# The first projection of a two-block layer: w_ada in whole rows, the context normed alone, x loaded last

## The chip, the cores and the metric

The kernel runs on one core of a Trainium2 chip. TensorE (PE, with weight loads PEld), VectorE (DVE), ScalarE (ACT) and GpSimd (POOL) each take their instructions in the order in which they were issued; SyncE (SP) issues most of the DMAs, ACT some. The metric is the device time of one execution in microseconds (us). The kernel before took 3486.61, 3495.49 and 3491.95 us in three runs, median 3491.95 us.

## The reference, cut to what matters

Two transformer blocks run on 512 tokens of width 1024. The first block has a context of 256 tokens beside x, and its norm is modulated by vectors that come from a matrix `w_ada`:

```python
def _modulate(x, g, shift, scale):
    return _rmsnorm(x, g) * (1 + scale) + shift

def _ada(cvec, w_ada, b_ada):                      # w_ada: 1024 x 6144
    mod = jax.nn.silu(cvec) @ w_ada + b_ada
    return jnp.split(mod, N_MOD, axis=-1)
...
    sh1, sc1, ga1, sh2, sc2, ga2 = _ada(c[:, None, :], w_ada, b_ada)
    csh1, csc1, ... = _ada(c_ctx, w_ada, b_ada)
    h, hc = _modulate(x, n, sh1, sc1), _modulate(ctx, n, csh1, csc1)
    ... = _split_in(h @ w_in);  ... = _split_in(hc @ w_in)
    dt_f = softplus(dt_raw[..., :32] + dtb_f)      # the scan's decays come from dt
    a_cs = cumsum(dt * A)                          # within chunks of 128
```

Then come neighbourhood attention, a bidirectional state-space scan (which starts from states of the context), 16 experts, and the second block with three kinds of attention and a gated MLP. All of it is fp32.

## The kernel before, in words

Everything is one program, and each engine's order is the order in which Python issues its instructions. Weights pass through a `Stream`: a raw tile (1 MB of `w_in`, two buffers, tag `raw`) is split into a high part `wh` (ACT, L199) and a low part `wl` (DVE or POOL, L219), in five pairs of buffers. The projection is a row of *steps*. A step is three matmuls (high by high, L330, low activation by high, L331, high by low weight, L332), and `st.fill(c)` issues steps until their costs add up to c: a context step costs 0.33, so `fill(1.0)` issues four and `fill(0.7)` three. `st.defer(n, f)` runs f after n more steps; `st.count` is the number of steps so far.

The stage that the change touches is the first:

- `ada_load` brings the first third of `w_ada` (columns 0 to 2047, 8 MB) as 16 tiles of 512 KB on SP's queue; eight buffers `aw`. The context (2 tiles) and x (4 tiles) come on ACT's queue into `xt`. ACT takes sums of squares (L655), DVE the reciprocal roots (L656, L515 to L520) and the products (L659), PE turns the tiles (L670), ACT and DVE copy them out to `cT` and `xT` (L676, L678).
- PE multiplies silu(c) with `w_ada` (L649). DVE copies the sum to `mod0` (L682), PE turns it (`ptm`, L886), DVE makes the shift and scale `shc`, `gsc` (L892 to L894).
- `modulate(v, ...)` (L683 to L693) makes for each of 8 blocks k: the scaled block (DVE, L686), its high part (ACT, L691: `c_hi`, `h_hi`) and its low part (L692: `c_lo`, `h_lo`). v is 1 for the context and 0 for x.
- Steps, in this order: `ub`, 32 steps of the context (`psc` into `bcT`, with a convolution: ACT L714, 8 DVE instructions L719 per half); `udt`, 8 steps of the context and 8 of x (`psg` into `dtT`); then `xc_unit(0)` to `xc_unit(3)`, 32 context steps each. So x is first needed at step 41.
- The second and last third of `w_ada` come in 16 loads of 1 MB (`ada_load2`, L857, on ACT's queue, three buffers), multiplied by `ada_mm2` (L865) every 10 steps from step 20 on; load i+3 is deferred by 8 steps after product i.
- `dt_ops` turns `dtT` (`dtn`, L759) and makes softplus and `n` = dt A in DVE's small instructions (L760 to L786), one per step; after 16 empty steps PE makes the running sums (`acs`, L766 to L768). For x the chain begins `SX` = 70 steps after `dtT`.

Of the kernel before, what the change touches and what calls it, by code (L numbers as in the profile page):

```python
# [544 lines left out]
ROT = "gsmgsms"  # L545
AQ = 20
AL = 8
SX = 70
VT_ = 't'
VD = 16  # L550
NG = 3
# [16 lines left out]
def first_block(kb, es, after):  # L568
    nc, tc, A = kb.nc, kb.tc, kb.A
    V, S, G, P = nc.vector, nc.scalar, nc.gpsimd, nc.tensor  # L570
# [11 lines left out]
    PS = kb  # L582
# [33 lines left out]
    cT = p0.tile([128, 8, TC], F32, name="cT")  # L616
    raw = ExitStack()
    p00 = raw.enter_context(tc.tile_pool(name="p00", bufs=1, side="right"))
    aw = {}

    def ada_load(kh):
        for j in range(4):
            t = p00.tile([128, 2, 512], F32, tag="aw", bufs=8, name="aw")
            nc.sync.dma_start(t, A["w_ada"][256 * kh:256 * kh + 256, 512 * j:512 * j + 512].rearrange("(k p) f -> p k f", p=128))
            aw[kh, j] = t

    ada_load(0)
    ada_load(1)
    xt = p00.tile([128, 6, D], F32, name="xt")
    for t in (4, 5, 0, 1, 2, 3):  # L630
        src = A["x"][128 * t:128 * t + 128] if t < 4 else A["ctx"][128 * (t - 4):128 * (t - 4) + 128]
        S.dma_start(xt[:, t], src)
    tri = p1.tile([128, 3, 128], F32, name="tri")
    sel = p1.tile([128, 18], F32, name="sel")
    dtv, acs, dte, Eac, cdec = (p1.tile([128, 6, 64], F32, name=n_) for n_ in "dtv acs dte Eac cdec".split())
# [7 lines left out]
    S.activation(sil[:, :, 0:2].rearrange("p k v -> p v k"), cols[:, 112:128].rearrange("p (v k) -> p v k", v=2), AF.Silu)  # L643
    ada_ps = PS.bank([128, 512], F32, "o", "ada")

    def ada_mm(kh):
        for k in range(2):
            for j in range(4):
                P.matmul(ada_ps[32 * j:32 * j + 32], sil[:, 2 * kh + k], aw[kh, j][:, k],  # L649
                         start=kh == 0 and k == 0, stop=kh == 3 and k == 1, skip_group_check=True)  # L650

    ss = p0.tile([128, 6], F32, name="ss")
    junk = xT[:, 0:2].rearrange("p a b -> p (a b)")
    for t in (4, 5, 0, 1, 2, 3):
        S.activation(junk, xt[:, t], AF.Square, accum_out=ss[:, t:t + 1])  # L655
    V.tensor_scalar(ss, ss, 1.0 / D, EPS, op0=ALU.mult, op1=ALU.add)  # L656
    rs = kb.rsqrt(ss, 6, p0)
    for t in (4, 5, 0, 1, 2, 3):
        V.tensor_scalar(xt[:, t], xt[:, t], rs[:, t:t + 1], None, op0=ALU.mult)  # L659
    ada_mm(0)  # L660
    ada_load(2)
    ada_mm(1)
    ada_load(3)
    S.dma_start(tri, A["tri"])
    S.dma_start(sel, A["sel"])
    for n in range(12):
        ps = PS.bank([128, 512], F32, "gsm"[n % 3], "xTp")
        for i in range(4):
            k, t = (2 * n + i // 2, 4 + i % 2) if n < 4 else (n - 4, i)
            P.transpose(ps[:, 128 * i:128 * i + 128], xt[:, t, 128 * k:128 * k + 128], ident)  # L670
        if n < 4:
            o, v = cT[:, 2 * n:2 * n + 2].rearrange("p a b -> p (a b)"), ps
        else:
            o, v = in_time(xT[:, n - 4]), ps.rearrange("p (r g c) -> p r g c", g=8, r=8)
        if n % 2:
            V.tensor_copy(o, v)  # L676
        else:
            S.activation(o, v, AF.Copy)  # L678
    ada_mm(2)
    ada_mm(3)  # L680
    mod0 = p0.tile([128, 512], F32, name="mod0")
    V.tensor_copy(mod0, ada_ps)  # L682
    raw.close()  # L683
    def modulate(v, src, hi, lo, each):
        def scale(k):
            V.tensor_scalar(src[:, k], src[:, k], gsc[:, v, k:k + 1], shc[:, v, k:k + 1], op0=ALU.mult, op1=ALU.add)  # L686
        scale(0)
        for k in range(8):
            if k < 7:
                scale(k + 1)  # L690
            S.activation(hi[:, k], src[:, k], AF.Copy)  # L691
            (G if k % 2 or v else V).tensor_tensor(lo[:, k], src[:, k], hi[:, k].bitcast(F32), op=ALU.subtract)  # L692
            each(k)  # L693


# [25 lines left out]
    def xbc_unit(c0, ch0, out, after):  # L721

        u = Unit([([(0, A["w_in"][512 * i:512 * i + 512, c0:c0 + 512])], 4) for i in range(2)], 512)
        ps = []

        def step(k, j):
            def fn(wh, wl):
                if k == 0 and j % 2 == 0:
                    ps.append(PS.bank([128, 512], F32, "g", "psc"))
                o = ps[-1][:, 256 * (j % 2):256 * (j % 2) + 256]  # L730
                w = slice(128 * j, 128 * j + 128)
                kb.mm3(o, wh[:, w], wl[:, w], *act_c(k), k == 0 and j % 2 == 0, k == 7, skip=True)
# [12 lines left out]
        return st.add(u)

    def dt_ops(t0, nt):

        n = 64 * nt
        tk = slice(t0, t0 + nt)  # L750
        b = {}
        tmp = lambda nm: px.tile([128, 256], F32, tag="dtt", bufs=5, name=nm)[:, :n]
        xr, na, u, d, s = (tmp(n_) for n_ in "x n u d s".split())
        th = lambda v: v.rearrange("p (t h) -> p t h", h=64)

        def turn():
            b["t"] = PS.bank([128, 512], F32, "m", "dtn")[:, :n]
            for t in range(nt):
                P.transpose(b["t"][:, 64 * t:64 * t + 64], dtT[:, 128 * (t0 + t):128 * (t0 + t) + 128], ident[:64, :64])  # L759
            tt(th(xr), th(b["t"]), dtb[:, None, :].to_broadcast([128, nt, 64]), op=ALU.add)  # L760

        def sums():
            ps = PS.bank([128, 512], F32, "m", "acs")
            pv, pt_ = [th(ps[:, 256 * i:256 * i + n]) for i in range(2)]
            a = th(na)
            P.matmul(pv[:, :, :32], tri[:, 0], a[:, :, :32], start=True, stop=True, skip_group_check=True)  # L766
            P.matmul(pv[:, :, 32:], tri[:, 1], a[:, :, 32:], start=True, stop=True, skip_group_check=True)
            P.matmul(pt_, tri[:, 2], a, start=True, stop=True, skip_group_check=True)  # L768
# [14 lines left out]
        ops += [lambda q=q: stt(d, d, 1.0 / q, u, op0=ALU.add, op1=ALU.mult) for q in (13, 11, 9, 7, 5, 3)]
        ops += [lambda: stt(d, d, 1.0, s, op0=ALU.add, op1=ALU.mult),
                lambda: stt(dtv[:, tk].rearrange("p t h -> p (t h)"), d, 2.0, xr, op0=ALU.mult, op1=ALU.add),
                lambda: stt(th(na), dtv[:, tk], -1.0, alog[:, None, :].to_broadcast([128, nt, 64]), op0=ALU.mult, op1=ALU.mult),  # L786
               ] + [None] * 16 + [
                sums, None, None,
                lambda: S.activation(dte[:, tk], dte[:, tk], AF.Exp)]
        return ops  # L790
# [87 lines left out]

    st.stop = True
    ub = xbc_unit(OB, 16, bcT, b_nat)  # L880
    st.add(udt)
    us = [xc_unit(0)]
    st.pump_some(1)
    ptm = PS.bank([128, 512], F32, "t", "ptm")
    for m in range(4):
        P.transpose(ptm[:, 128 * m:128 * m + 128], mod0[:, 128 * m:128 * m + 128], ident)  # L886
    shc = p0.tile([128, 2, 8], F32, name="shc")
    gsc = p0.tile([128, 2, 8], F32, name="gsc")
    for v in (1, 0):
# [2 lines left out]
        V.tensor_tensor(shc[:, v].rearrange("p (j m) -> p j m", m=4), pv[:, 0:2], b4[:, 0], op=ALU.add)  # L892
        V.tensor_tensor(gsc[:, v].rearrange("p (j m) -> p j m", m=4), pv[:, 2:4], b4[:, 1], op=ALU.add)
        V.scalar_tensor_tensor(gsc[:, v], gsc[:, v], 1.0, cols[:, 0:8], op0=ALU.add, op1=ALU.mult)  # L894
    for i in range(3):
        ada_load2(i)
    modulate(1, cT, c_hi, c_lo, lambda k: k in (1, 3, 5) and st.pump_some(1))
    st.stop = False
    st.wait = WAIT
# [2 lines left out]
    kb.rot = ["g", "s"]  # L902
    st.defer(ADA0, lambda: ada_mm2(0))
    S.activation(alog, alog, AF.Exp)
    modulate(0, xT, h_hi, h_lo, lambda k: st.fill(1.0))
    zero.close()
    for g in range(1, 4):
        us.append(xc_unit(g))
# [1718 lines left out]
```

## Time and profile before

| | before |
|---|---|
| median of three runs | 3491.95 us |
| profiled execution, its own time | 3494.57 us |
| its span | 3492.8 us |
| PE busy in the span | 3237.3 us (93%) |
| first 140 us: PE's first projection step | 41.64 us |
| last matmul of the dt unit's x part starts | 72.97 us |
| acs sums of x start | 140.04 us |

Times count from the start of the span. A timeline row has start, duration, engine, line, operation, output<-inputs, the shape and how often (rows that follow each other are merged); what stands in brackets is the idle time before it on that engine and what ended it. A matmul's duration includes its way through the array, so rows overlap: the distance between starts is the pace. In rows of the first `w_ada` product, of the products L865 and of the sums L766 to L768 one matmul of the program is recorded as two. In a row of windows the columns are: window, its length, busy time of PE, PEld, DVE, ACT, POOL (with instructions), TensorE's granted clock as a share of 2.4 GHz, the busy share of the DMA engines and GB/s.

### The profile page before, as it was taken

Reading aid. Unit: us, or ns where it says so; the run is one execution under the profiler, and the core shown is the slowest. Engines: PE = TensorE matmul, PEld = TensorE weight load, DVE = VectorE, ACT = ScalarE, POOL = GpSimd, SP = SyncE. Lnnn points to the kernel's source line nnn. Section 1 sums busy time; section 2 is a strip of 40 time slices with the busy share of each in tenths; the row PEclk is TensorE's granted clock in tenths of the full one; section 3 lists DMA queues with packets and bytes.
Section 4 is the critical chain, followed back from the end, with each engine's and each line's share of the span. In section 5 each row is a group of like instructions: output and inputs, shape, how many; then the busy total and the mean of one; then the engine's idle time right before and its main releaser. Section 6 shows DMA issues by size and latency. Waiting matters only on the chain. (4 is left out here: it accounts for less than half of the span.)

```text
span 3492.8 us, 42198 instructions
## 1 busy us (share of the span) xinstructions
PE 3237.3 (93%) x16445; PEld 2215.0 (63%) x16445; DVE 1631.3 (47%) x3097; ACT 1171.2 (34%) x2066; POOL 568.5 (16%) x380
## 2 busy tenths in 40 slices
PE   7899999999999698988889887999999999999998
PEld 4678876666677443323324223777888877788887
DVE  5745556666554401110111004686544557755444
ACT  4455545454322100000000002554433345543332
POOL 2232213333211100000000002141111103401110
PEclk9999999999999799999999998999999999999999
DMA  8622131222344599999999995211232322123222
GB/s 295 226 64 81 55 97 64 76 79 73 115 163 152 219 403 418 420 421 421 421 421 421 421 421 231 80 46 52 87 95 93 106 72 69 40 67 111 91 87 82
DMA packets 222405, 642.45 MB, mean 184 GB/s; under 512 B 17889, under 2 KB 110169, under 8 KB 170749
## 3 DMA queue, kind: packets, MB, share of 16 engines
q1 hardware_dynamic: 208576, 600.89, 45.2%
q10 hardware_dynamic: 13629, 38.85, 3.1%
q8 instruction: 130, 2.13, 0.2%
q14 instruction: 70, 0.57, 0.1%
HBM read 625.52 MB, written 14.16 MB: 183 GB/s over the span
## 5 line engine op out<-in xcount | busy, mean ns | idle before, releaser
L1911 PE MATMUL hd<-xw,xe 128*64 128x512 f32 x2048 | 464.8, 597 | 63.0 <-DMA xw<-in_w_up_dram 41.7
L219 DVE TENSOR_TENSOR wl<-raw,wh 128x1024 fp32r<-128x1024 f32 (+1 forms) x301 | 372.9, 1253 | 134.3 <-ACT wh L199 129.7
L199 ACT ACTIVATE wh<-raw 128x1024 fp32r<-128x1024 f32 (+1 forms) x349 | 343.2, 1004 | 213.5 <-PE psg L332 131.5
L331 PE MATMUL psg<-HB,wh 128*128 128x512 f32 (+1 forms) x1024 | 388.5, 379 | 8.2 <-DVE HB L429 8.1
L330 PE MATMUL psg<-HA,wh 128*128 128x512 f32 (+1 forms) x1024 | 392.7, 384 | 0.0
L332 PE MATMUL psg<-HA,wl 128*128 128x512 f32 (+1 forms) x1024 | 388.1, 379 | 0.0
L1911 PEld LDWEIGHTS hd<-xw,xe 128*64 128x64 f32 x2048 | 151.1, 137 | 365.8 <-issue 245.2
L1952 PE MATMUL down<-xw,hidT 128*64 128x512 f32 x1024 | 236.5, 596 | 37.8 <-DMA xw<-in_w_down_dram 37.7
L330 PE MATMUL psg<-h_hi,wh 128*128 128x512 f32 x584 | 256.5, 439 | 0.9 <-DVE vsb L1288 0.8
L331 PE MATMUL psg<-h_lo,wh 128*128 128x512 f32 x584 | 237.2, 406 | 1.3 <-POOL h_lo L692 1.3
L332 PE MATMUL psg<-h_hi,wl 128*128 128x512 f32 x584 | 237.3, 406 | 0.0
L331 PEld LDWEIGHTS psg<-HB,wh 128*128 128x128 f32 x1024 | 195.3, 191 | 43.6 <-DVE HB L429 9.8
L332 PEld LDWEIGHTS psg<-HA,wl 128*128 128x128 f32 x1024 | 195.2, 191 | 35.8
L330 PEld LDWEIGHTS psg<-HA,wh 128*128 128x128 f32 x1024 | 195.8, 191 | 33.7
L1952 PEld LDWEIGHTS down<-xw,hidT 128*64 128x64 f32 x1024 | 74.9, 136 | 188.1 <-issue 119.2
L2539 POOL TENSOR_TENSOR va<-va,ga 128x512 f32<-128x512 f32 x44 | 91.2, 2073 | 552.9 <-DVE va L2521 552.6
L1967 ACT ACTIVATE yh<-down,gcol 128x512 fp32r<-128x512 f32 x16 | 11.0, 686 | 489.1 <-PE down L1952 489.1
L219 POOL TENSOR_TENSOR wl<-raw,wh 128x1024 fp32r<-128x1024 f32 (+1 forms) x48 | 113.1, 2360 | 378.7 <-ACT wh L199 378.4
L1923 DVE TENSOR_TENSOR hid<-hid,hd 128x512 f32<-128x512 f32 x32 | 22.0, 688 | 315.6 <-PE hd L1911 315.4
L1985 POOL TENSOR_TENSOR Y<-Y,R 128x512 f32<-128x512 f32 x8 | 9.9, 1273 | 970.8 <-ACT tmp L1984 970.8
L330 PEld LDWEIGHTS psg<-h_hi,wh 128*128 128x128 f32 x584 | 110.9, 190 | 54.0 <-issue 24.2
L332 PE MATMUL psg<-wh,hidl 128*128 128x512 f32 x352 | 139.2, 396 | 0.0
(479 smaller groups left out, 6043.1 us busy)
## 6 DMA issues: line engine op xcount, KB each, us to landing
xw<-in_w_gate_dram SPq DMA_DIRECT2D x128, 1024.0 KB, 19.8
xw<-in_w_up_dram SPq DMA_DIRECT2D x128, 1024.0 KB, 19.8
xw<-in_w_down_dram SPq DMA_DIRECT2D x126, 1024.0 KB, 19.8
raw<-in_w_up_dram SPq DMA_DIRECT2D x176, 256.0 KB, 3.9
raw<-in_w_in_dram SPq DMA_DIRECT2D x34, 1024.0 KB, 5.1
raw<-in_w_in_dram SPq DMA_DIRECT2D x96, 256.0 KB, 3.1
raw<-in_w_down_dram SPq DMA_DIRECT2D x44, 512.0 KB, 3.7
raw<-in_w_in_dram SPq DMA_DIRECT2D x33, 512.0 KB, 5.6
```

Of the source, the lines that this page charges most:

```text
L199: nc.scalar.activation(wh[:, :kn, :nco], src, AF.Copy)
L219: eng.tensor_tensor(wl[:, :kn, :nco], src, wh[:, :kn, :nco].bitcast(F32), op=ALU.subtract)
L330: nc.tensor.matmul(ps, l, r, start=first, stop=False, skip_group_check=skip)
L331: nc.tensor.matmul(ps, l, rh, start=False, stop=False, skip_group_check=skip)
L332: nc.tensor.matmul(ps, lh, r, start=False, stop=last, skip_group_check=skip)
L1911: P.matmul(ps[c][64 * e:64 * e + 64], xe[p // 2][k // 2 % 2][:, 2 * (k // 4) + k % 2, c0:c0 + 64], self.tiles[p, w, k, e][:, 512 * c:512 * ...
L1923: V.tensor_tensor(acts[p, c], acts[p, c], ps[c], op=ALU.mult)
L1952: P.matmul(down[h][64 * e:64 * e + 64], b[:, 64 * e:64 * e + 64], w[:, 1024 * r + 512 * h:1024 * r + 512 * h + 512], start=j == 0 and r == ...
L1967: S.activation(hi, down[h], AF.Copy, scale=gates[p])
L1985: G.tensor_tensor(o, o, R3[:, 512 * h:512 * h + 512], op=ALU.mult)
L2539: G.tensor_tensor(v, v, g[j], op=ALU.mult)
```

## The change

The tiles of `w_ada` become whole rows: eight loads of 1 MB with 8 KB runs, six buffers, all on SP's queue, and their product follows the turning of the context. Only the context is loaded ahead (ACT's queue) and normed alone. x is loaded on SP's queue behind the first two raw tiles of `w_in`, into two of the three buffers of `ada_load2`. Its squares stand on ACT behind the modulation of the context; the norm (`row_norm`), the turning (`x_turn`, one bank of the two with tag `m`) and the copies stand between context steps, and `modulate` of x comes behind all of them. `ada_load2(1)` and `(2)` are issued behind the last `x_turn`. Two groups of 5 and 9 small matmuls (`warm`) stand ahead of the first step. The low part of the context alternates between DVE and POOL. x's dt chain begins 56 steps after `dtT`, and 38 empty steps stand ahead of its sums.

```diff
-SX = 70
+SX = 56
...
-    ada_load(0)
-    ada_load(1)
-    xt = p00.tile([128, 6, D], F32, name="xt")
-    for t in (4, 5, 0, 1, 2, 3):
-        S.dma_start(xt[:, t], src)
+    xt = p00.tile([128, 2, D], F32, name="xt")
+    def ada_load(k):
+        aw.append(p00.tile([128, 4, 512], F32, tag="aw", bufs=6, name="aw"))
+        nc.sync.dma_start(aw[k], A["w_ada"][128 * k:128 * k + 128, :2048].rearrange("p (j f) -> p j f", f=512))
+    for k in range(6):
+        ada_load(k)
+    for t in range(2):
+        S.dma_start(xt[:, t], A["ctx"][128 * t:128 * t + 128])
...
+    row_norm([xt[:, t] for t in range(2)], 4, 2)
...
+    for k in range(8):
+        for j in range(4):
+            P.matmul(ada_ps[32 * j:32 * j + 32], sil[:, k], aw[k][:, j], start=k == 0, stop=k == 7, skip_group_check=True)
+        if k < 2:
+            ada_load(6 + k)
+    kb.warm("m", 5)
+    def x_turn(k):
+        ps = PS.bank([128, 512], F32, "m", "xTp")
+        for t in range(4):
+            P.transpose(ps[:, 128 * t:128 * t + 128], xx[t][:, 128 * k:128 * k + 128], ident)
+        ...  # copied to xT[:, k] by DVE for odd k, by ACT for even k
...
-            (G if k % 2 or v else V).tensor_tensor(lo[:, k], src[:, k], hi[:, k].bitcast(F32), op=ALU.subtract)
+            (G if k % 2 else V).tensor_tensor(lo[:, k], src[:, k], hi[:, k].bitcast(F32), op=ALU.subtract)
...
-               ] + [None] * 16 + [
+               ] + [None] * (16 if t0 else 38) + [
...
     ub = xbc_unit(OB, 16, bcT, b_nat)
+    xx = []
+    for t in range(4):
+        if t % 2 == 0:
+            xa = px.tile([128, 4, 512], F32, tag="aw", bufs=3, name="xa").rearrange("p (t a) c -> p t (a c)", t=2)
+        xx.append(xa[:, t % 2])
+        nc.sync.dma_start(xx[t], A["x"][128 * t:128 * t + 128])
     st.add(udt)
...
+    kb.warm("m", 9)
...
-    for i in range(3):
-        ada_load2(i)
+    ada_load2(0)
     modulate(1, cT, c_hi, c_lo, lambda k: k in (1, 3, 5) and st.pump_some(1))
...
-    modulate(0, xT, h_hi, h_lo, lambda k: st.fill(1.0))
+    for t in range(4):
+        S.activation(junk, xx[t], AF.Square, accum_out=ss[:, t:t + 1])
+        st.fill(0.7)
+    row_norm(xx, 0, 4)
+    for k in range(8):
+        x_turn(k)
+        st.fill(0.6)
+    ada_load2(1)
+    ada_load2(2)
+    modulate(0, xT, h_hi, h_lo, lambda k: st.fill(0.6))
```

The order on ACT in the projection's first part, before, from the last high parts of the context on (`h_hi` is x's high part; `aw` the later thirds of `w_ada`):

```order
L691 ACTIVATE c_hi<-cT 128x256 x2
L904 ACT_TABLE_LOAD
L904 ACTIVATE alog<-alog 128x64
L691 ACTIVATE h_hi<-xT 128x512 x4
L199 ACTIVATE wh<-raw 128x1024
L714 ACTIVATE bcT<-psc,cols,cw 128x256 x2
```

The same place now, to x's first high parts (`xa` is x, `xTp` its turned blocks):

```order
L694 ACTIVATE c_hi<-cT 128x256 x2
L913 ACT_TABLE_LOAD
L913 ACTIVATE alog<-alog 128x64
L915 ACTIVATE xT,ss<-xa 128x1024 x4
L683 ACTIVATE xT<-xTp 128x8x8x8
L199 ACTIVATE wh<-raw 128x1024
L717 ACTIVATE bcT<-psc,cols,cw 128x256 x2
L683 ACTIVATE xT<-xTp 128x8x8x8
L199 ACTIVATE wh<-raw 128x1024
L683 ACTIVATE xT<-xTp 128x8x8x8
L199 ACTIVATE wh<-raw 128x1024
L683 ACTIVATE xT<-xTp 128x8x8x8
```

The four squares of x and the four copies now stand between the context's high parts and x's. ACT's next rows now (`aw` are loads of the later thirds, `bcT` the output of `ub`):

```order
L199 ACTIVATE wh<-raw 128x1024
L860 DMA aw_507<-in_w_ada_dram 128x2048
L860 DMA aw_509<-in_w_ada_dram 128x2048
L860 DMA aw_511<-in_w_ada_dram 128x2048
L694 ACTIVATE h_hi<-xT 128x512 x2
L717 ACTIVATE bcT<-psc,cols,cw 128x256 x2
L741 ACT_TABLE_LOAD
L741 ACTIVATE bcT<-bcT 128x1024
L199 ACTIVATE wh<-raw 128x1024
L694 ACTIVATE h_hi<-xT 128x512 x3
```

Three loads of `w_ada` stand behind the last copy and one more split of a raw tile; between x's second and third high part stand the convolution of `ub`'s second half, a table load, a silu and a split.

On PE the eight turnings of x stand between the steps of `ub`. The first comes behind 12 steps, and the last is followed by four steps and the product that reads `aw_509` (the second of the three loads above):

```order
L678 MATMUL xTp<-ident,xa 128x128 x4
L330 MATMUL psc<-c_hi,wh 128x256
L331 MATMUL psc<-c_lo,wh 128x256
L332 MATMUL psc<-c_hi,wl 128x256
L330 MATMUL psc<-c_hi,wh 128x256
L331 MATMUL psc<-c_lo,wh 128x256
L332 MATMUL psc<-c_hi,wl 128x256
L678 MATMUL xTp<-ident,xa 128x128 x4
```

Two steps stand between each two turnings. Before, PE's program began thus (`pt` are small vectors), and all 48 transposes of context and x came in one piece ahead of the second half of the product:

```order
L637 MATMUL pt<-ident,va 128x128
L638 MATMUL pt<-ident,vb 128x120
L649 MATMUL ada<-aw,sil 32x512 x16
L670 MATMUL xTp<-ident,xt 128x128 x48
L649 MATMUL ada<-aw,sil 32x512 x16
L886 MATMUL ptm<-ident,mod_290 128x128 x4
```

What moved is x's 32 transposes, from ahead of the product's second half into the steps. In DVE's order x's dt chain, before, is spread over a convolution, products for the context's states and a split:

```order
L783 SCALAR_TENSOR_TENSOR d_624<-d_624,u_623 128x256 x4
L839 TENSOR_TENSOR xd_1131<-xn_1126,ddc_297 128x512
L839 TENSOR_TENSOR xd_1133<-xn_1126,ddc_297 128x512
L784 SCALAR_TENSOR_TENSOR d_624<-d_624,s_625 128x256
L785 SCALAR_TENSOR_TENSOR dtv_127<-d_624,x_621 128x256
L839 TENSOR_TENSOR xd_1158<-xn_1153,ddc_297 128x512
L839 TENSOR_TENSOR xd_1160<-xn_1153,ddc_297 128x512
L786 SCALAR_TENSOR_TENSOR n_622<-dtv_127,alog_303 128x256
```

Now it ends ahead of them:

```order
L786 SCALAR_TENSOR_TENSOR d_640<-d_640,u_639 128x256 x6
L787 SCALAR_TENSOR_TENSOR d_640<-d_640,s_641 128x256
L788 SCALAR_TENSOR_TENSOR dtv_119<-d_640,x_637 128x256
L789 SCALAR_TENSOR_TENSOR n_638<-dtv_119,alog_233 128x256
L219 TENSOR_TENSOR wl_1104<-raw_1042,wh_1103 128x1024
```

From the turning of x's dt to the first `acs` matmul PE's order has 113 rows before and 180 now (some 22 steps more).

## Rows read from the trace of the kernel before

**Rows 1.** Waits of PE from 0 to 140 us: total, times, longest.
```profile
PE psc L331 <- POOL c_lo L692: 2.7, 5, 1.0
PE acs L766 <- DVE n L786: 7.0, 1, 7.0
```

**Rows 2.** Timeline of PE: the end of the first product, the first step.
```profile
35.11 1.90 PE L649 MATMUL ada<-aw,sil 128*32 128x512 f32 x10 [1.49 <-DMA aw<-in_w_ada_dram]
41.64 0.58 PE L330 MATMUL psc<-c_hi,wh 128*128 128x256 f32 x1 [3.19 <-ACT c_hi L691]
```

**Rows 3.** Windows of the first 35 us.
```profile
0.00:5.00 5.00, 0.00 (x0) 0.00 (x0) 0.00 (x0) 0.00 (x0) 0.19 (x4) 1.00 0.60 184
5.00:10.00 5.00, 0.91 (x2) 0.36 (x2) 0.75 (x3) 0.00 (x0) 0.00 (x0) 1.00 1.04 397
30.00:35.00 5.00, 3.62 (x28) 1.20 (x26) 1.20 (x2) 0.60 (x1) 0.00 (x0) 1.00 1.06 388
```

**Rows 4.** Timeline of ACT: squares, last context part, table load, alog.
```profile
11.84 1.28 ACT L643 ACT_TABLE_LOAD   x1 [11.84 <-DMA xt<-in_ctx_dram]
14.42 1.06 ACT L655 ACTIVATE xT<-xt 128x1024 f32<-128x1024 f32 x1
15.60 1.06 ACT L655 ACTIVATE xT<-xt 128x1024 f32<-128x1024 f32 x1
51.72 0.42 ACT L691 ACTIVATE c_hi<-cT 128x256 fp32r<-128x256 f32 x1 [1.72 <-DVE cT L686]
53.46 0.26 ACT L904 ACTIVATE alog<-alog 128x64 f32<-128x64 f32 x1
```

**Rows 5.** Timeline of DVE: the norm, mod0, one convolution.
```profile
20.72 0.17 DVE L656 TENSOR_SCALAR ss<-ss 128x6 f32<-128x6 f32 x1 [12.42 <-ACT xT L655]
23.14 4.07 DVE L659 TENSOR_SCALAR xt<-xt,rs_y 128x1024 f32<-128x1024 f32 x6
37.05 0.69 DVE L682 COPY mod<-ada 128x512 f32<-128x512 f32 x1 [5.67 <-PE ada L649]
59.55 3.98 DVE L719 SCALAR_TENSOR_TENSOR bcT<-psc,cw,bcT 128x255 f32<-128x255 f32 x8 [0.23 <-ACT bcT L714]
```

**Rows 6.** Timeline of POOL and PE: block 5's low part, a product, two matmuls.
```profile
48.83 0.73 POOL L692 TENSOR_TENSOR c_lo<-cT,c_hi 128x256 fp32r<-128x256 f32 x1 [0.68 <-ACT c_hi L691]
55.44 1.06 PE L865 MATMUL ada<-aw,sil 128*32 128x512 f32 x8
54.05 0.28 PE L331 MATMUL psc<-c_lo,wh 128*128 128x256 f32 x1
54.17 0.28 PE L332 MATMUL psc<-c_hi,wl 128*128 128x256 f32 x1
```

**Rows 7.** One line's DMAs (L857, 30 to 110 us).
```profile
DMA to landing us min/median/max: 6.1/6.8/9.1
```

**Rows 8.** Timeline of ACT, DVE, POOL, PE: silu, x's blocks, turnings, dt's end.
```profile
75.38 1.28 ACT L738 ACT_TABLE_LOAD   x1 [4.13 <-DVE bcT L719]
76.68 1.06 ACT L738 ACTIVATE bcT<-bcT 128x1024 f32<-128x1024 f32 x1
64.02 0.64 ACT L691 ACTIVATE h_hi<-xT 128x512 fp32r<-128x512 f32 x1 [3.03 <-DVE xT L686]
63.45 0.54 DVE L686 TENSOR_SCALAR xT<-xT,gsc,shc 128x512 f32<-128x512 f32 x1
54.84 1.28 POOL L692 TENSOR_TENSOR h_lo<-xT,h_hi 128x512 fp32r<-128x512 f32 x1 [1.66 <-ACT h_hi L691]
78.76 0.60 PE L817 MATMUL bct<-ident,bcT 128*128 128x128 f32 x4
72.97 0.41 PE L332 MATMUL psg<-h_hi,wl 128*128 128x512 f32 x1
```

**Rows 9.** Windows: steps from 75.6 us on, then the sums of x.
```profile
75.60:94.00 18.40, 17.70 (x143) 14.30 (x141) 14.15 (x28) 11.71 (x15) 7.15 (x3) 1.00 0.94 340
140.04:143.00 2.96, 2.96 (x12) 2.78 (x13) 2.85 (x6) 0.00 (x0) 0.00 (x0) 0.50 0.23 44
```

More of the change, by code (lines that the diff above doesn't have):

```diff
@@ L618, in first_block @@
     p00 = raw.enter_context(tc.tile_pool(name="p00", bufs=1, side="right"))
[L619 to L625, printed above, removed]
-    ada_load(0)
-    ada_load(1)
-    xt = p00.tile([128, 6, D], F32, name="xt")
-    for t in (4, 5, 0, 1, 2, 3):
-        src = A["x"][128 * t:128 * t + 128] if t < 4 else A["ctx"][128 * (t - 4):128 * (t - 4) + 128]
-        S.dma_start(xt[:, t], src)
+    xt = p00.tile([128, 2, D], F32, name="xt")
+    aw = []
+    def ada_load(k):
[5 more added lines that the diff above has]
+        S.dma_start(xt[:, t], A["ctx"][128 * t:128 * t + 128])
     tri = p1.tile([128, 3, 128], F32, name="tri")
@@ L644, in first_block @@
     ada_ps = PS.bank([128, 512], F32, "o", "ada")
[L646 to L650, printed above, removed]
     ss = p0.tile([128, 6], F32, name="ss")
     junk = xT[:, 0:2].rearrange("p a b -> p (a b)")
-    for t in (4, 5, 0, 1, 2, 3):
-        S.activation(junk, xt[:, t], AF.Square, accum_out=ss[:, t:t + 1])
@@ L656, in first_block, with row_norm @@
[L656 to L663, printed above, removed]
+    for t in range(2):
+        S.activation(junk, xt[:, t], AF.Square, accum_out=ss[:, 4 + t:5 + t])
     S.dma_start(tri, A["tri"])
     S.dma_start(sel, A["sel"])
-    for n in range(12):
+    def row_norm(x, t0, n):
+        v = ss[:, t0:t0 + n]
+        V.tensor_scalar(v, v, 1.0 / D, EPS, op0=ALU.mult, op1=ALU.add)
+        rs = kb.rsqrt(v, n, p0)
+        for t in range(n):
+            V.tensor_scalar(x[t], x[t], rs[:, t:t + 1], None, op0=ALU.mult)
@@ L667, in first_block @@
+    row_norm([xt[:, t] for t in range(2)], 4, 2)
+    for n in range(4):
         ps = PS.bank([128, 512], F32, "gsm"[n % 3], "xTp")
         for i in range(4):
[L669 to L672, printed above, removed]
-        else:
-            o, v = in_time(xT[:, n - 4]), ps.rearrange("p (r g c) -> p r g c", g=8, r=8)
@@ L675, in first_block @@
-        if n % 2:
+            P.transpose(ps[:, 128 * i:128 * i + 128], xt[:, i % 2, 256 * n + 128 * (i // 2):256 * n + 128 * (i // 2) + 128], ident)
+        o = cT[:, 2 * n:2 * n + 2].rearrange("p a b -> p (a b)")
+        if n % 2:
+            V.tensor_copy(o, ps)
+        else:
+            S.activation(o, ps, AF.Copy)
+    for k in range(8):
[3 more added lines that the diff above has]
+            ada_load(6 + k)
@@ L676, in first_block @@
+    kb.warm("m", 5)
[3 more added lines that the diff above has]
+            P.transpose(ps[:, 128 * t:128 * t + 128], xx[t][:, 128 * k:128 * k + 128], ident)
+        o, v = in_time(xT[:, k]), ps.rearrange("p (r g c) -> p r g c", g=8, r=8)
+        if k % 2:
             V.tensor_copy(o, v)
@@ L678, in first_block @@
             S.activation(o, v, AF.Copy)
-    ada_mm(2)
-    ada_mm(3)
     mod0 = p0.tile([128, 512], F32, name="mod0")
```

## The prediction

> **What bounds the kernel now.** The page's engine shares give PE 93% of the span, so I read first where PE waits. The waits of PE up to 140 us say that it waited 7.0 us in one place, for DVE's last instruction of x's dt chain, and 2.7 us in five places for the context's low parts [rows 1]. The timeline of PE shows the start: the first product of `w_ada` still waits for a DMA at 35.11, and the first projection step starts at 41.64, behind ACT's first high part [rows 2]. The windows show why: from 5 us on the DMAs move 388 to 397 GB/s [rows 3], so until 35 us the queues are the limit, and x's 2.1 MB are among their bytes. The reader should see that x's squares and turnings cost nothing there, because PE waits for `w_ada` anyway. From 75.6 us on PE is busy 17.7 of 18.4 us [rows 9], and its list of waits has little else until the 7 us. What matters is thus how much earlier the steps start, whether x is ready when its steps come, and whether the wait at 133 us goes.
>
> I count the chain from M, the start of DVE's copy `mod0`: 37.05 us [rows 5]. From there the order up to the context's last high part is nearly the same in both kernels.
>
> **Part 1: the start.** x's four tiles (2.1 MB) no longer go ahead of `w_ada`; at 388 GB/s [rows 3] that is 5.4 us. Against it stands a new wait: loads 7 and 8 need the buffers of the first two products, and these come behind the context's norm and its 16 transposes. The context has landed by 11.84 at the latest (ACT's table load was let go then) [rows 4]; two squares at 1.18 us (the distance of two of them) [rows 4] take 2.4, DVE's twelve small instructions 2.4 and two products at 0.68 (4.07 over 6) 1.4 [rows 5], four groups of transposes 2.4 (0.60 each [rows 8]) and the first product 1.1 [rows 6]: load 7 is issued at 21.5. Six tiles, the context and the small loads are 7.75 MB; 0.92 MB are through at 5 us and 397 GB/s from then on [rows 3], so the queue runs empty at 22.2. A load that takes 6.1 us at best [rows 7], 2.7 of it for its megabyte, leaves it empty for up to 2.7 us, or not at all. I take half of that: M comes 4.0 us earlier (2.7 to 5.4), at 33.0.
>
> The rate in rows 3 was reached with 512 KB issues, eight in flight. The Trainium skill (DMA: Bandwidth & Descriptors, Bandwidth) counsels batches of 1 MiB and more and gives 425 GB/s for one long transfer. By that rate the 9.8 MB would be there about 2 us earlier, and the sum below would be 2 us less; the trace has shown no such rate in this stretch, and I keep its own.
>
> **Part 2: x's path.** ACT's order decides it. The context's last high part ends at 52.14, which is M+15.1, and `alog` at M+16.7 [rows 4]; both rest on the same alternation of splits, scalings and high parts as now, and giving DVE every second low part leaves that alternation as it is. Behind `alog` stand x's four squares, 4.7 us: M+21.4. DVE then needs 2.4 us for the small instructions and 4 x 0.68 = 2.7 for the products: M+26.5. PE, meanwhile, has 12 steps. They need the low parts of blocks 0 to 5; block 5's was ready at 49.56 [rows 6], M+12.5, so PE is done at about M+13 and waits some 13 us in front of the first turning, a wait that wasn't there. (x itself lands in time: two raw tiles, x and one load of `aw` are 5.2 MB, at 388 GB/s 13.5 us from about M on, and the squares can't start before M+16.7. The tile of the dt unit, now queued on SP behind x, is used on ACT only behind x's first copy.) The small matmuls ahead of the first step only fill time in which PE waits.
>
> The loop has 8 turnings at 0.60 [rows 8], 16 steps at 0.35 (three matmuls 0.117 apart) and one product of 1.06 [rows 6], 11.5 us. After the wait of 7 us the granted clock stood at 0.50 for 3 us [rows 9], which cost half of them; after 13 us I put 1.5 us down for it, and 0.5 for the turning that finds its bank not yet emptied, since DVE's convolution of 3.98 us [rows 5] stands between two copies. The loop ends at M+40.
>
> Then comes a second new wait. The loads of `aw` for the second and third product are issued on ACT behind a split that waits for the loop's last step (1.04 more) and behind a load for the fourth product: the one that PE needs next goes out at M+41.5, and PE stands in front of its product at M+40.7. A load takes 6.1 to 9.1 us, median 6.8 [rows 7]; with one megabyte ahead of it I take 8.0 (6.1 to 11.8, which is 9.1 and the 2.7 of the other). PE goes on at M+49.5. Product and two steps, at half clock, are 2 us: M+51.5. ACT's half of the convolution takes 0.5, DVE's 3.98 [rows 5]: M+56. On ACT table load, silu and split come first, 1.28 + 1.06 + 1.04 = 3.4 [rows 8, 2 to 4], then x's third high part, 0.64 [rows 8]: M+60. For the remaining blocks DVE has per pair two scalings of 0.54 [rows 8] and a low part, taken as 0.69 from the copy of the same shape [rows 5]: 1.8; three pairs 5.4, and POOL ends with a low part of 1.28 [rows 8]. The last matmul of the dt unit starts at about M+67.
>
> Before, it started at 72.97, M+35.9 [rows 8]. So x's path costs 31.3 us, of which the earlier M takes off 4.0: **+27.3**. PE can't cover this: only 40 steps, 14 us, don't need x, and all else stands behind in PE's order.
>
> **Part 3: the decays.** x's chain starts 14 steps earlier and the sums stand 22 steps later behind its start, at 0.35 about 8 us more room than before, when DVE was 7.0 late [rows 1]. That wait goes; with it the 3.0 us at half clock behind it, 1.5 us [rows 9]. DVE's work stays the same and is now ahead of the convolution. **-8.5**, bounded by 0 (DVE as late as before, since it too was held up) and -8.5.
>
> **Part 4: what is caught up.** Behind the dt unit PE had 0.7 us idle in 18.4 [rows 9]; little can be made good there. I take **-1.5** (0 to -3). Behind 140 us nothing changes but the time at which it starts.
>
> **Sum.** 27.3 - 8.5 - 1.5 = +17.3 on the profiled execution's own 3494.57 us: 3511.9. That execution stood 2.6 us above the median of the runs, 3491.95; against the median the time is **3509 us**. The bounds: M from 2.7 to 7.4 us earlier (the last by the faster queue), the load from 6.1 to 11.8, the clock's 3 us or none, the rest as above: +9 to +25, 3501 to 3517.
>
> **Rivals.**
> A. x is in time, and the change is faster. If neither new wait shows, the start brings 4.0, the decays 8.5 and the five waits for low parts 2.7 [rows 1], and the 32 transposes add 4.8 to PE: -10.4, 3482 us. For it speaks that x lands early and that DVE and ACT have idle time in the stretch; against it ACT's order, in which the squares can't start before M+16.7. It decides from the point at which the two waits together stay under some 10 us; I count 13 and 9, and x's late high parts on top.
> B. The second wait is short: if the load lands in 6.1 us and the two scalings and POOL's parts run beside the silu, x is ready about 10 us sooner: +7, 3499 us. For it: the first load in its queue is the fourth product's, and it may have landed by then. Against: the convolution, the table load and the silu stay in front.
> C. The decays bring nothing: DVE, held up by the convolutions behind the dt unit, is late for the sums as before. +26, 3518 us. For it speaks DVE's 14.2 busy of 18.4 us in the stretch [rows 9]; against it that its chain now stands ahead of that work.
>
> **How the numbers follow.** Forecast 0.62, A 0.12, B 0.16, C 0.10. 0.3% (10.5 us) is what a measurement of this kernel can tell from no change. The forecast lies above +10.5 for 0.55 of its 0.62; B for 0.05; C wholly: slower 0.70. No change: 0.07 of the forecast, 0.11 of B, 0.04 of A, 0.22. Faster: the rest of A, 0.08. The range from 3490 to 3519 holds the forecast, B and half of C; the forecast's own is 3501 to 3517.
>
> **What would show it.** In the profile after: first step at about 37.6 (M+4.6); PE idle some 13 us in front of the first `xTp`, put down to DVE's product of x; a wait of some 9 us for `aw` in front of the second product L868; the last matmul of the dt unit at about 100 us; no wait of 7 us in front of `acs`, and the sums of x at about 162 us. I am wrong if ACT's squares run earlier than the context's last high part, if the product doesn't wait for its load, or if the wait for `acs` is still there.

## The result and the profile after

The changed kernel took 3514.46 us (median of four runs, 3512.76 to 3518.72) against 3491.15 us for the kernel before (3486.61 to 3495.49): 0.69% slower, ratio 1.0069, 95% interval 1.0056 to 1.0082. The forecast of 3509 us was 5.5 us too low. The profiled execution took 3518.72 us (span 3516.8), 24.15 us more than that of before.

The waits of PE from 0 to 180 us (total, times, longest) answer to [rows 1]:

```profile
PE xTp L678 <- DVE xa L656: 11.1, 3, 10.7
PE ada L868 <- DMA aw<-in_w_ada_dram: 7.8, 1, 7.8
PE psg L330 <- ACT h_hi L694: 3.6, 1, 3.6
PE psg L331 <- DVE h_lo L695: 1.9, 1, 1.9
PE xn L838 <- ACT xc L741: 2.4, 2, 2.0
PE psc L332 <- POOL wl L219: 1.8, 1, 1.8
PE psc L331 <- DVE c_lo L695: 1.1, 1, 1.1
```

The wait of 7.0 us for `acs` is gone, and no row is left for it. In its place stand the two forecast waits, 10.7 us in front of x's first turning and 7.8 us in front of the second product of `aw`, and behind them two that the forecast had not priced apart: 3.6 us for x's third high part and 1.9 us for its low part.

The windows of the start (columns as in [rows 3]), and one further on:

```profile
0.00:5.00 5.00, 0.00 (x0) 0.00 (x0) 0.00 (x0) 1.28 (x1) 0.19 (x4) 1.00 0.62 216
5.00:10.00 5.00, 0.45 (x1) 0.18 (x1) 0.00 (x0) 0.00 (x0) 0.00 (x0) 1.00 1.02 414
10.00:15.00 5.00, 0.46 (x1) 0.18 (x1) 0.75 (x3) 1.26 (x3) 0.00 (x0) 1.00 1.02 410
15.00:20.00 5.00, 0.00 (x0) 0.00 (x0) 2.22 (x13) 1.15 (x2) 0.00 (x0) 1.00 1.02 422
20.00:25.00 5.00, 4.26 (x24) 3.41 (x28) 2.42 (x4) 1.20 (x2) 0.00 (x0) 1.00 0.24 87
97.00:102.00 5.00, 4.78 (x11) 3.19 (x11) 4.76 (x7) 1.71 (x3) 2.58 (x2) 0.50 0.86 297
```

From 5 to 20 us the queues run faster than in [rows 3], at 410 to 422 GB/s for 397, and then they have next to nothing to move from 20 to 25 us (87 GB/s). ACT's and DVE's timelines show why, and where M (the copy `mod0`) now stands:

```profile
13.02 1.04 ACT L646 ACTIVATE xT<-xt 128x1024 f32<-128x1024 f32 x1
16.19 1.06 ACT L646 ACTIVATE xT<-xt 128x1024 f32<-128x1024 f32 x1 [2.03 <-DMA xt<-in_ctx_dram]
36.81 1.06 ACT L199 ACTIVATE wh<-raw 128x1024 fp32r<-128x1024 f32 x1 [12.35 <-DMA raw<-in_w_in_dram]
94.11 1.14 ACT L694 ACTIVATE h_hi<-xT 128x512 fp32r<-128x512 f32 x2
33.94 0.69 DVE L685 COPY mod<-ada 128x512 f32<-128x512 f32 x1 [8.82 <-PE ada L670]
37.90 1.23 DVE L219 TENSOR_TENSOR wl<-raw,wh 128x1024 fp32r<-128x1024 f32 x1 [3.27 <-ACT wh L199]
```

The context's second tile lands near 16 us; in before both had landed by 11.84 [rows 4]. The norm, the turnings and the first two products, which free the buffers for the last two loads, come later by that. SP's own waits say the same:

```profile
SPq L624 <- PE ada L670: 9.7, 2, 9.3
```

PE's timeline reads as follows; the first row answers to [rows 2], and the others follow x's path to its end.

```profile
40.71 0.38 PE L330 MATMUL psc<-c_hi,wh 128*128 128x256 f32 x1 [3.08 <-ACT c_hi L694]
59.37 1.05 PE L678 MATMUL xTp<-ident,xa 128*128 128x128 f32 x2 [10.72 <-DVE xa L656]
82.42 1.08 PE L868 MATMUL ada<-aw,sil 128*32 128x512 f32 x4 [7.81 <-DMA aw<-in_w_ada_dram]
94.77 0.51 PE L330 MATMUL psg<-h_hi,wh 128*128 128x512 f32 x1 [3.58 <-ACT h_hi L694]
97.22 0.80 PE L331 MATMUL psg<-h_lo,wh 128*128 128x512 f32 x1 [1.94 <-DVE h_lo L695]
104.62 0.42 PE L332 MATMUL psg<-h_hi,wl 128*128 128x512 f32 x1
```

The last row is the end of the dt unit: 31.65 us later than in before [rows 8]. The whole is 24.15 us longer, so 7.5 us come back behind it; they come back within this stage, since its last PE work (the last `stc` of the table below) is 23.7 us later.

### The profile page after: what moved, and what is told of

Its sections match the earlier page's. It is cut to its first block, busy times and chain, and to the rows that moved or that the text cites. A ratio compares the mean times of both kernels' runs of the same rounds, so it can differ in the third digit from the quotient of the medians.

```text
span 3516.8 us, 42242 instructions
## 1 busy us (share of the span) xinstructions
PE 3240.3 (92%) x16473; PEld 2220.3 (63%) x16473; DVE 1626.6 (46%) x3113; ACT 1169.9 (33%) x2064; POOL 561.3 (16%) x376
## 5 line engine op out<-in xcount | busy, mean ns | idle before, releaser
L332 PEld LDWEIGHTS psg<-HA,wl 128*128 128x128 f32 x1024 | 195.0, 190 | 35.9
```

The costliest lines, as they stand in the source:

```text
L332: nc.tensor.matmul(ps, lh, r, start=False, stop=last, skip_group_check=skip)
```

## The experiments

Twelve kernels ran, each at least five times. The ratio is to the kernel before, run on the same chip in the same series. The last column is the start of the last product of the context's states (`stc`, the last PE work of this stage) in the profiled execution, of which there is one for each kernel. Behind it all kernels run the same program, for 3293 to 3301 us, while whole runs of one kernel differ by up to 14 us. How much the last two columns scatter was not measured apart, but after, e2, e3, e4, e6, e10 and e12 have the same program up to `mod0`, and it starts between 33.9 and 35.5 us in them: differences of 1 to 2 us there say little. Differences to after are given between medians of different series; by the ratios they are up to 3.5 us larger or smaller.

| kernel | median, us | ratio to before (95%) | mod0 at | last stc at |
|---|---|---|---|---|
| before | 3488.73 to 3491.70 (four series) | 1 | 37.1 | 192.7 |
| after | 3514.46 | 1.0069 (1.0056 to 1.0082) | 33.9 | 216.4 |
| e1 decays alone | 3486.18 | 0.9989 (0.9981 to 0.9998) | 37.4 | 187.0 |
| e2 decays undone | 3519.73 | 1.0094 (1.0081 to 1.0106) | 35.5 | 224.0 |
| e3 products late | 3510.23 | 1.0058 (1.0045 to 1.0071) | 34.6 | 211.7 |
| e4 x's dt behind ctx | 3516.15 | 1.0074 (1.0062 to 1.0086) | 34.5 | 216.5 |
| e5 context first | 3510.01 | 1.0052 (1.0040 to 1.0064) | 29.3 | 210.6 |
| e6 turnings late | 3515.00 | 1.0068 (1.0056 to 1.0080) | 34.1 | 212.7 |
| e7 decays, low parts | 3483.77 | 0.9980 (0.9971 to 0.9990) | 37.2 | 185.5 |
| e8 rows alone | 3499.82 | 1.0022 (1.0014 to 1.0031) | 44.4 | 198.3 |
| e9 = e3 and e5 | 3503.64 | 1.0040 (1.0027 to 1.0053) | 29.6 | 207.2 |
| e10 x not normed | 3504.88 | 1.0049 (1.0035 to 1.0062) | 34.9 | 205.1 |
| e11 short runs | 3516.57 | 1.0073 (1.0060 to 1.0086) | 32.8 | 214.3 |
| e12 as e4, sums kept | 3515.45 | 1.0072 (1.0059 to 1.0084) | 35.0 | 215.8 |

### The decays: e1 and e2

e1, on the kernel before:

```diff
-SX = 70
+SX = 56
...
-               ] + [None] * 16 + [
+               ] + [None] * (16 if t0 else 38) + [
```

> The kernel before with only the move of x's decays (SX 56, 38 empty steps ahead of x's sums). Theory: PE's wait of 7.0 us in front of the sums goes, with the 3 us at half clock behind it: 6 to 8.5 us less than before, 3483 to 3485 us, and no wait above 1 us in front of acs. Rival: DVE is held up by its convolutions and is as late as before, or the wait comes back elsewhere: 3490 to 3493 us.

e2, on the kernel after: the same two lines back.

> The kernel after with x's decays put back (SX 70, 16 empty steps). Theory: the wait in front of x's sums is there again, 5 to 7 us with half clock behind it: after plus 5 to 8.5 us, 3519.5 to 3523 us. Rival: PE's waits ahead of the dt unit have given DVE the time it lacked, so the sums come in time anyway: 3513 to 3516 us.

e1 is 0.11% faster (ratio 0.9989; 3486.18 for 3490.31 us), its last `stc` 5.7 us earlier. e2 is 5.3 us above after, its last `stc` 7.6 us later, of which 1.6 are there at `mod0` already. In e2 the wait stands in front of the sums as before, and as long:

```profile
PE acs L769 <- DVE n L789: 7.0, 1, 7.0
```

So the theory's mechanism holds in both kernels and e2's rival falls: PE's waits ahead of the dt unit give DVE no time, since its chain begins behind them. The size is 4 to 6 us (4.1 and 5.3 by the medians, 5.7 and 6.0 at the last `stc`) and not 8.5, though e2's ratio taken alone would give 8.7. The waits of e1 behind 76 us show what takes a part back:

```profile
PE xn L835 <- ACT xc L738: 3.1, 2, 2.0
PE psc L332 <- POOL wl L219: 1.8, 1, 1.8
PE psg L331 <- DVE wl L219: 1.4, 1, 1.4
```

In before PE waited 1.1 us for `xc` and not at all for POOL's `wl` there. With PE no longer held up 7 us, these two come late by 2.0 and 1.8 us more. DVE's `wl` costs less than before; its 1.4 us in e1 lie behind the last `stc`.

### The start: e5, e11, e8

e5, on after: `va`, `vb` and the context go to SP's queue, ahead of `w_ada`.

```diff
-    S.dma_start(va, A["vec_a"])
-    S.dma_start(vb, A["vec_b"])
+    nc.sync.dma_start(va, A["vec_a"])
+    nc.sync.dma_start(vb, A["vec_b"])
...
+    for t in range(2):
+        nc.sync.dma_start(xt[:, t], A["ctx"][128 * t:128 * t + 128])
     for k in range(6):
         ada_load(k)
-    for t in range(2):
-        S.dma_start(xt[:, t], A["ctx"][128 * t:128 * t + 128])
```

> The kernel after with the two small loads va and vb and the context moved from ACT's queue to SP's, ahead of w_ada. Theory: the context landed late (second tile near 16 us) because the 8 KB rows of w_ada on the other queue took the rate; with it first in the same queue it is there by 8 us, the first two products free their buffers before the queue runs dry, and the stretch at 87 GB/s (20 to 25 us) goes: mod0 starts 3 to 5 us earlier than 33.9, and the whole is 2.5 to 5 us shorter than after, 3509.5 to 3512 us. Rival: the megabyte ahead of w_ada costs as much as the dry stretch, or mod0 comes earlier and x, behind ACT's and DVE's work, does not: 3513.5 to 3516 us.

The theory held: the context's first square starts at 5.86 us and its second at 7.21, the dry stretch is gone, `mod0` comes 4.6 us earlier and the time is 4.5 us below after. What `va` and `vb` have in it, which moved with the context and stand ahead of its squares, was not taken apart. ACT's timeline and the window that was dry:

```profile
7.21 1.06 ACT L646 ACTIVATE xT<-xt 128x1024 f32<-128x1024 f32 x1 [0.19 <-DMA xt<-in_ctx_dram]
```

```profile
20.00:25.00 5.00, 3.00 (x16) 0.36 (x16) 0.00 (x0) 0.00 (x0) 0.00 (x0) 0.70 1.01 421
```

The waits of 10.7, 7.5 and 3.6 us behind it are those of after: the chain from M on moves as a whole.

e11, on after: shorter runs in four times as many loads, all else the same.

```diff
-        nc.sync.dma_start(aw[k], A["w_ada"][128 * k:128 * k + 128, :2048].rearrange("p (j f) -> p j f", f=512))
+        for j in range(4):
+            nc.sync.dma_start(aw[k][:, j], A["w_ada"][128 * k:128 * k + 128, 512 * j:512 * j + 512])
```

> The kernel after with each of the eight w_ada loads cut into four of 256 KB (runs of 2 KB instead of 8 KB), same tiles, same queue, same order. Theory: the long runs on SP's queue took the rate from ACT's; with short ones va lands by 6 us instead of 8.9, the context by 12 to 14 instead of 16, the loads 7 and 8 are issued earlier and the stretch at 87 GB/s shrinks: mod0 1.5 to 3 us earlier and the whole 1 to 3 us below after, 3511.5 to 3513.5 us. Rival: the six megabytes queued ahead matter and not the run length: va at 8.9 us and mod0 at 34 as in after, 3514 to 3517 us.

Half right. PE gets `va` at 5.24 us, and the context's second square starts at 11.88 instead of 16.19, so the way SP's loads are cut decides who is served; the packets in the last section speak for the length of the runs and not the number of loads. But the total rate falls, and takes most of it back:

```profile
5.00:10.00 5.00, 0.91 (x2) 0.36 (x2) 0.75 (x3) 1.86 (x3) 0.00 (x0) 1.00 0.94 329
15.00:20.00 5.00, 3.56 (x16) 3.24 (x16) 2.45 (x6) 1.04 (x2) 0.00 (x0) 1.00 1.05 375
20.00:25.00 5.00, 5.00 (x42) 1.27 (x43) 0.69 (x1) 0.16 (x1) 0.00 (x0) 1.00 0.99 353
```

`mod0` is 1.1 us earlier and the last `stc` 2.1, hardly more than the scatter, and the whole time, 3516.57 us, can't be told from after.

e8, on before: only `w_ada` in whole rows, four buffers of 1 MB for eight of 512 KB.

```diff
+        aw.append(p00.tile([128, 4, 512], F32, tag="aw", bufs=4, name="aw"))
+        nc.sync.dma_start(aw[k], A["w_ada"][128 * k:128 * k + 128, :2048].rearrange("p (j f) -> p j f", f=512))
...
+    for k in range(4):
+        ada_load(k)
...
+            if k < 4:
+                ada_load(4 + k)
```

> The kernel before with only the loads of w_ada changed: eight of 1 MB in whole rows (8 KB runs), four buffers, SP's queue; x and the context on ACT's queue and normed together, as before. Theory: w_ada's rows take the rate from ACT's queue, the context and x land later than before (x's last tile by 4 us or more) and the norm, the turnings and with them the loads 5 to 8 come later: mod0 at 38 to 42 instead of 37.1, the whole 1 to 4 us above before, 3491.5 to 3494.5 us. Rival: the total rate is what counts, and it is higher (410 to 420 GB/s for 397): mod0 1 us earlier, 3489 to 3490 us.

The mechanism was right and its size too small: 0.22% slower, 8 us. ACT's row of the square of x's last tile shows it; in before it started at 19.54 us.

```profile
27.51 1.06 ACT L654 ACTIVATE xT<-xt 128x1024 f32<-128x1024 f32 x1 [2.62 <-DMA xt<-in_x_dram]
```

The norm waits for all six tiles, the products for the norm and the loads 5 to 8 for the products: `mod0` is 7.3 us later. Whole rows alone are thus a loss in this order of work, though the rate from 5 to 30 us is 410 to 423 GB/s.

### x's path: e10, e3, e9, e6, e4, e12

e10, on after:

```diff
     for t in range(4):
-        S.activation(junk, xx[t], AF.Square, accum_out=ss[:, t:t + 1])
         st.fill(0.7)
-    row_norm(xx, 0, 4)
```

> The kernel after without x's four squares, reciprocal roots and products: x goes into its turnings as it is loaded (that part of the computation is left out). Theory: the wait of 10.7 us in front of the first turning is these 9.8 us on ACT and DVE, and all of x's path behind it moves up as a whole: after minus 8 to 11 us, 3503.5 to 3506.5 us, with the first xTp at 49 to 51 us and the waits for the load and for h_hi as in after. Rival: the convolution, the load or the splits hold x's path anyway, and the waits behind grow by what is saved: 3511 to 3515 us.

The first turning starts at 49.5 us instead of 59.4, the last `stc` is 11.3 us earlier and the time 9.6 us below after. The waits behind stay:

```profile
PE ada L868 <- DMA aw<-in_w_ada_dram: 7.8, 1, 7.8
PE psg L330 <- ACT h_hi L694: 2.4, 1, 2.4
PE psg L331 <- DVE h_lo L695: 2.1, 2, 1.9
```

So the norm of x on ACT and DVE, behind the context's high parts, costs its full length (10 us), and nothing on the way makes it good. This shows the forecast's first wait directly, and that it is on the path.

e3, on after:

```diff
-ADA = 10
-ADA0 = 20
+ADA = 9
+ADA0 = 36
...
-AL = 8
+AL = 7
```

> The kernel after with the first product of the second third of w_ada at step 36 instead of 20 and the next ones every 9 steps instead of 10 (loads 7 steps behind a product instead of 8). Theory: PE no longer stands 7.8 us in front of a load; the convolution, the silu and x's third high part come as much earlier: after minus 6 to 9 us, 3505.5 to 3508.5 us. Rival: x's high and low parts are late by ACT's and DVE's own work, and the waits of 3.6 and 1.9 us for h_hi and h_lo grow by what the load gave: 3512 to 3515 us.

Between the two: 4.2 us below after, the last `stc` 4.7 us earlier. The wait for the load is gone, but two others grew:

```profile
PE psg L330 <- ACT h_hi L694: 6.5, 1, 6.5
PE ada L868 <- DVE modx L871: 3.8, 1, 3.8
PE psg L331 <- DVE h_lo L695: 1.7, 1, 1.7
```

```profile
86.99 1.14 ACT L694 ACTIVATE h_hi<-xT 128x512 fp32r<-128x512 f32 x2
```

The convolution and x's third high part came 7 us earlier (86.99 for 94.11), and the dt unit ended at 97.52 instead of 104.62: 7.1 us, as the theory said for x's path. PE reached its place 10 us earlier, x's part was ready 7 us earlier, so the wait for `h_hi` grew by 3. The later place of the products then cost 3.8 us in front of the last third's first product, whose bank DVE copies out late (`modx`).

e9 is e3 and e5 in one kernel.

> e5_ctx_first and e3_products_late together. Theory: the late context (4.5 us) and the wait for the load in x's loop (4.2 us) are separate, and their gains add: 3505 to 3507 us, still some 22 us above e7, which is what is left of x's late path. Rival: the second only moved because x was late by the first, and together they bring little more than one: 3509 to 3511 us.

3503.64 us, 10.8 below after, last `stc` 9.2 us earlier where the sum of the two is 10.5: they nearly add. 20 us are left over e7; x's norm, which e10 takes out, is half of that, and what the rest is was not taken apart.

e6, on e3:

```diff
-        st.fill(0.7)
+        st.fill(2.0)
...
         x_turn(k)
-        st.fill(0.6)
+        st.fill(0.3)
```

> The kernel of e3_products_late with 28 steps instead of 12 ahead of the first turning of x, and one step instead of two behind each turning. Theory: the 10.7 us in front of the first turning are ACT's and DVE's (the squares behind the context's high parts, the norm, the products); PE can fill 5.6 us of them with steps, and x's path behind them is 5 to 6 us shorter: 5 to 8 us less than e3, 3502 to 3505.5 us; the wait in front of the first xTp falls from 10.7 to about 5 us. Rival: the turnings were paced by DVE's and ACT's copies and not by the steps between them, and the wait for h_hi (6.5 us in e3) grows by what PE saves: 3508 to 3511.5 us.

My theory fell. The first turning comes at 68.2 us, 8.8 later than in after, behind a wait of 12.2 us. ACT's and DVE's rows show what the steps brought with them:

```profile
62.68 1.06 ACT L199 ACTIVATE wh<-raw 128x1024 fp32r<-128x1024 f32 x1 [2.94 <-DMA raw<-in_w_in_dram]
```

```profile
56.84 3.98 DVE L722 SCALAR_TENSOR_TENSOR bcT<-psc,cw,bcT 128x255 f32<-128x255 f32 x8 [6.85 <-ACT bcT L717]
60.73 2.51 DVE L219 TENSOR_TENSOR wl<-raw,wh 128x1024 fp32r<-128x1024 f32 x1
63.78 1.23 DVE L219 TENSOR_TENSOR wl<-raw,wh 128x1024 fp32r<-128x1024 f32 x1 [0.53 <-ACT wh L199]
64.92 0.16 DVE L653 TENSOR_SCALAR ss<-ss 128x4 f32<-128x4 f32 x1
```

A step isn't PE's alone: issued between the squares, 28 of them put a convolution and the splits of the next weights on ACT and DVE ahead of the norm, and one split waits 2.9 us for its raw tile. The rival had a part in it too: with one step between two turnings, PE waited 4.1 and 2.4 us for DVE's and ACT's copies. The last `stc` is 1.0 us behind e3's, the median 4.8, so there is no gain by either, and how much is lost stays open. PE's idle time couldn't be filled by steps that use the engines for which it waited.

e4, on after: x's eight steps in a unit of their own behind `xc_unit(0)`; e12 is e4 with `SX = 24`.

```diff
+    udx = Unit([([(0, A["w_in"][:, ODT:ODT + 128])], 8)], 128)
...
-    kb.group_b(udt, 0, act_t, T, ev_dtx)
+    kb.group_b(udx, 0, act_t, T, ev_dtx)
...
     us = [xc_unit(0)]
+    st.add(udx)
```

> The kernel after with x's 8 steps of the dt unit put behind the context steps of xc_unit(0) (with a load of their weights of their own), so that x is first needed at step 73 instead of 41. Theory: the waits for h_hi (3.6 us) and h_lo (1.9 and 0.4 us) and the half clock there go: after minus 6 to 9 us, 3505.5 to 3508.5 us; the waits of 10.7 and 7.8 us stay. Rival: the waits only move, to the sums of x or to the convolutions of xc_unit(0) that x's low parts now meet on DVE: 3512 to 3517 us.

> As e4_x_dt_behind_ctx, but x's chain begins 24 steps behind dtT instead of 56, so that x's sums stand at the same step as in after (in e4 they came 32 steps later). Theory: with x first needed at step 73 the waits for h_hi and h_lo go and nothing takes their place: 3506 to 3509 us. Rival, which e4 spoke for: x's scalings and low parts meet the context's dt chain on DVE, PE waits some 5 us for dtT instead, and x's sums lose the room they had: 3513 to 3518 us.

(In both, the states of the context's first group take their decays before the last two products on these are made; the work is the same.) The rival was right: 3516.15 and 3515.45 us, no gain. The waits for x's parts go, but PE stands in front of the context's dt instead, because DVE's copy `dtT` is queued behind x's scalings and low parts and a convolution:

```profile
PE dtn L762 <- DVE dtT L804: 4.7, 1, 4.7
```

### A version that beats both: e7

On e1:

```diff
-            (G if k % 2 or v else V).tensor_tensor(lo[:, k], src[:, k], hi[:, k].bitcast(F32), op=ALU.subtract)
+            (G if k % 2 else V).tensor_tensor(lo[:, k], src[:, k], hi[:, k].bitcast(F32), op=ALU.subtract)
```

> The kernel before with x's decays moved (as e1_decays_alone) and the context's low parts alternating between DVE and POOL. Theory: PE's five waits of 2.7 us in all for c_lo go, a part of them is spent on waits for c_hi instead: 1 to 2.5 us less than e1, 3483.5 to 3485 us, the fastest here. Rival: ACT's high parts bound the first steps, and c_hi takes the waits over: 3486 us, as e1.

3483.77 us, 0.20% below before (ratio 0.9980, interval 0.9971 to 0.9990), as forecast and the fastest here. It keeps the two parts of the change that take work off a late engine and leaves the order of the loads alone. That it beats e1 rests on 1.5 us at the last `stc` and 1.4 at the context's last high part (50.7 us for 52.1); the runs' intervals overlap.

## Why the prediction was right, and where it was off

Right were the sign, the mechanism and most of the times along the chain.

1. *Part 1, the start: the size held by luck.* M came 3.1 us earlier, forecast 4.0; in the six other kernels with the same start it came 1.6 to 3.0 us earlier, mostly less than the 2.7 of the lower bound. The step "the context has landed by 11.84 at the latest" failed: I took the landing of before, though six loads with 8 KB runs now stood on the other queue. Its second tile came near 16, the last two loads were issued behind waits of 9.3 and 0.4 us, and the queue was empty for some 5 us where I had put down 1.35. The faster rate (410 to 422 GB/s) paid for a part of it. e5 shows that the late context (with `va` and `vb`) cost 4.6 us, e11 with its packets that the run length made it late.
2. *First step: wrong.* It came at 40.71 (M+6.8), not M+4.6, since DVE's first split of a raw tile (37.90) stands ahead of the shift and scale, and that tile, issued behind the last load of `w_ada`, landed only at 36.8. The alternation of low parts on DVE and POOL, for which I had put nothing down, made about half of this good: from M to the context's last high part e7 takes 1.2 us less than e1, which differs from it in this alone. That high part ended at M+16.0, forecast M+15.1.
3. *x's path: right to the third high part.* The wait in front of the first turning was 10.7 us (13), PE reached the product at 82.42 after 7.8 us (82.5 after 9), and the third high part began at M+60.2 (over at M+60).
4. *The end of x's path: too short.* From the end of that part to the last dt matmul I put 7 us; it took 9.9. I took 0.69 us for a low part on DVE and 0.54 for a scaling; the first low part took 2.42, beside POOL's `wl`, and PE waited 1.9 us for it, and the next scalings took 1.95 for two and 1.52 for one, beside low parts on POOL (below). In before a scaling beside POOL's low part took 1.53 us too, at 54.88, but my sum went by the row of 0.54. Behind that wait PE had half its clock: 0.50 of 2.4 GHz from 97 to 102 us, a second stretch that the sum didn't have. With M's 0.9 us, and 0.7 by which the third high part was over late, this is +31.65 at the end of dt for the +27.3 of the forecast. (The forecast's subtraction was 0.2 us off as well: M+67 less M+35.9 is 31.1, not 31.3.)
5. *Parts 3 and 4: too much.* I put 10 us down, 7.5 came back. The 7.0 us wait went, as did the half clock behind it, but e1 shows some 4 us of new waits for ACT's `xc` and POOL's `wl`, partly set off by shorter ones for DVE's. "That wait goes" was right; that nothing is late next was not.

The sum: 17.3 + 4.35 + 2.5 = 24.15 us on the profiled execution; by the medians it is 23.3. Rival A fell because both waits showed, B because the load took as long as forecast, C because the wait for the sums is gone. The Trainium skill's rate for long transfers (DMA: Bandwidth & Descriptors, Bandwidth), which I left out of the sum, was nearer to the trace: 410 to 422 GB/s from 5 to 20 us where that page has 425 for one transfer of 16 MB. Taken with nothing else it would have made the forecast worse, since the starved context stood against it.

## What to carry to other kernels

A tensor that is loaded last drags its whole preparation behind whatever the preparing engines have queued: count it there, not on the engine that is busy most, and check how much independent work the busy engine has by then (here 14 us against 31). Steps put into one engine's wait don't help if they also use the engines for which it waits (e6). When a wait is taken away, look for what would be late next: here about a third of the gain went there (some 6 us of 8.5 were left in e1).

## What the runs showed of the hardware

- Run length on one queue decides how fast the other is served. With 8 KB runs on SP's queue, PE could start on the 64 KB load `va` on ACT's queue at 8.88 us, with 2 KB runs (e11, the same tiles in four loads each) at 5.24; the total rate from 5 to 20 us was 410 to 422 GB/s for 329 to 390. The profile's DMA rows give each queue's packets, MB and share of the engines' time; q1 is SP's queue and q10 ACT's. From 2 to 8 us, first after, then e11:

```profile
q1 hardware_dynamic: 288, 2.12, 86.5%
q10 hardware_dynamic: 283, 0.13, 7.5%
q1 hardware_dynamic: 615, 1.13, 59.4%
q10 hardware_dynamic: 553, 0.68, 32.6%
```

  The two queues were served nearly packet for packet, and one of SP's held 7.4 KB in after and 1.8 KB in e11 (MB over packets), so the length of the runs set what was left for ACT. It isn't one for one throughout: from 8 to 15 us after has 234 packets on SP's queue and 420 on ACT's. The Trainium skill (DMA: Bandwidth & Descriptors, Queues, rings and completion order) says that an engine goes round the queues a packet of descriptors at a time, which fits the stretch from 2 to 8 us; whether its packets are those of the profile, no run here shows.
- A low part on DVE (two inputs from SBUF) that began while POOL worked on a split took 2.42 us, 0.69 by itself. After's POOL and DVE rows:

```profile
94.28 2.35 POOL L219 TENSOR_TENSOR wl<-raw,wh 128x1024 fp32r<-128x1024 f32 x1 [15.08 <-ACT wh L199]
94.75 2.42 DVE L695 TENSOR_TENSOR h_lo<-xT,h_hi 128x512 fp32r<-128x512 f32 x1 [3.47 <-ACT h_hi L694]
99.86 1.28 POOL L695 TENSOR_TENSOR h_lo<-xT,h_hi 128x512 fp32r<-128x512 f32 x1 [1.55 <-ACT h_hi L694]
99.89 1.52 DVE L689 TENSOR_SCALAR xT<-xT,gsc,shc 128x512 f32<-128x512 f32 x1
```

  POOL's ended at 96.63 and DVE's at 97.17, 0.54 us later, as if it had run only then. The Trainium skill (SBUF — State Buffer, SBUF: two separate sides) calls the port pair of the two an exclusive lock; the trace agrees, here and in e12 (2.44 us at the same place). DVE's scaling, with one tile as input, was late beside POOL as well: 1.52 us for 0.54, over 0.27 us behind POOL's low part.
- Behind its waits of 3.6 and 1.9 us PE had half its clock (0.50, 1.2 GHz) from 97 to 102 us, while it was busy 4.78 of 5.00 us.
